# Opening of a fused two-model kernel: tokens loaded in two layouts, norms carried by the transform's table, modulation units in pairs, one order for the tensor engine

## The chip, the core and the metric

The kernel runs on one core of a Trainium2 chip. The metric is the device time of one whole execution, in microseconds (us). Smaller is better. The core has a tensor engine (PE), whose weight loads are listed apart as PEld, a vector engine (DVE), a scalar engine (ACT), GpSimd (POOL) and a sync engine (SP) that issues most transfers. Each engine works through its own queue of instructions in order.

## The reference

Two models run one after the other in single precision on a latent stream of 256 tokens and a context of 256 tokens, 1024 channels wide. The change touches the first layer of the first model only:

```python
silu_c, silu_cc = silu(c), silu(c_ctx)              # conditioning vectors, one per stream
for i in range(4):                                  # layers: fourier, diff attention, MLA, fourier
    sh_a, sc_a, g_a, sh_m, sc_m, g_m = split(silu_c @ mod_w[i] + mod_b[i], 6)     # csh_a ... from silu_cc
    h_lat = rms_norm(x_lat, norm_mix_g[i]) * (1 + sc_a) + sh_a                     # the context alike
    y_lat = mixer(h_lat)    # i = 0: real(fft2 over tokens and groups of 256 channels) @ fourier_w + bias
    x_lat = x_lat + g_a * y_lat
    h = rms_norm(x_lat, norm_mlp_g[i]) * (1 + sc_m) + sh_m
    x_lat = x_lat + g_m * (square(relu(h @ mlp_w1[i])) @ mlp_w2[i])
# then a second model: two layers of a state-space mixer beside attention, each with an MLP
```

## The kernel before

Activations lie with channels on the 128 partitions and the 512 tokens of both streams in columns (`self.x[k]`, k = 0 to 7). Every product of single precision is made of three products of rounded parts: a number is split into `hi` (a rounded cast on ACT) and `lo` (the rest, on DVE), and PE adds hi times hi, hi times lo and lo times hi. `split` (L396) does so for activations, `loadw` for weights: one transfer of 1 MB into a `raw` buffer (three of these), issued by SP at L288, then two casts `whi` on ACT (L306) and two rests `wlo` on DVE (L307). `whi` and `wlo` have five buffers each, the general tiles `g` 41, the accumulators `mm` and `aux` in PSUM four each.

**Modulation units.** The vectors sh_a to g_m of layer 0 are 24 units of 256 numbers for both streams: 0 to 3 are sh_a, 4 to 7 sc_a, 8 to 11 g_a, 12 to 15 sh_m, 16 to 19 sc_m, 20 to 23 g_m. `mod_land` loads 1 MB for a unit, into a `raw`, `whi`, `wlo` or `g` buffer. `mod_a` makes eight matmuls (L545, 16 records in the trace) into `aux` and lets ACT copy the result to `modsb` (L548). `mod_b` transposes it on PE (L556), and DVE sums it (L559) and adds the bias (L563). `mod_units` does the products of one unit ahead of the second half of the unit before. Units 20 to 23 are fed in among the MLP's first work. The other layers' vectors are made on DVE instead, by `mod_rows`: a row of silu(c) times a row of weights, summed (L588), beside PE's work; `rows_silu` makes that row first.

**The opening**, `start` (L883 to 1037). SP issues tokens, the first table, units 4 to 7, the second table and units 0 to 3. Each token's mean square is taken on ACT (L913); the normalised tokens are split (ACT L922, DVE L923); PE transposes the raw tokens into `self.x` (32 transposes, L930). The first transform is 96 matmuls (L946), whose sums are copied to `g` tiles (L951, L953). Then PE runs the eight units. Then ACT and DVE scale by 1 + sc_a and split (L980, L981), GpSimd writes two more columns for the shift sh_a (L976 for hi, L977 for lo), and PE makes the second transform (L995), 96 matmuls. Fourier weight tiles follow, units 8 to 11, 16 to 19 and 12 to 15, the last four output tiles in halves (`tail`), the norm, and the MLP's `head`, in which DVE makes one normalised tile for each k (L639, L643) and PE follows it with matmuls (L674 to 676). A plain `linear` (L324) is next.

A scheduler sets each engine's order, from the text and its own estimate of when operands are ready. `issue_after` forbids it to place work ahead of a named instruction.

Of the kernel before, what the change touches and what calls it, by code (L numbers as in the profile page):

```python
# [17 lines left out]
P = 128  # L18
# [105 lines left out]
def prep(inp):  # L124
    f = {k: np.asarray(v) for k, v in inp.items()}
    o = dict(_constants())
    o["xtok"] = np.concatenate([f["x"][0], f["ctx"][0]], axis=0).reshape(4, P, 2, 512).transpose(0, 2, 1, 3)
    o["cT"] = np.ascontiguousarray(
# [4 lines left out]
        DEPTH - 1, 24, P, 2 * D)  # L133
    o["mod_b"] = np.concatenate([_vecT(f["mod_b"][l]) for l in range(DEPTH)], axis=1)
# [107 lines left out]
class Body:  # L242
# [324 lines left out]
    def mod_units(self, units, dst, where="r"):  # L567

        prev = None
        for i, uu in enumerate(units):  # L570
            sb = self.mod_a(self.mod_land(uu, where[i % len(where)]))
            if prev:
                self.mod_b(*prev, dst)
            prev = (uu, sb)
            yield
        self.mod_b(*prev, dst)

    def mod_rows(self, l, ns, dst):


        nc = self.nc
        for cpt in (1, 0, 2, 4, 3, 5):
            for u in range(4):
                r = self.raw(self.I["mod_wT"][l - 1, cpt * 4 + u], 2048)
                c0 = cpt * 8 + u * 2
                for j in range(2):
                    for s in range(ns[cpt]):
                        nc.vector.tensor_tensor_reduce(  # L588
                            out=self.junk, in0=r[:, D * j:D * j + D], in1=self.silu_b[:, D * s:D * s + D],
                            scale=1.0, scalar=0.0, op0=ALU.mult, op1=ALU.add, accum_out=dst[:, c0 + j, s:s + 1])  # L590
                nc.vector.tensor_tensor(
                    out=dst[:, c0:c0 + 2, :ns[cpt]], in0=dst[:, c0:c0 + 2, :ns[cpt]],
                    in1=self.modb[:, l * 48 + c0:l * 48 + c0 + 2].unsqueeze(2).to_broadcast([P, 2, ns[cpt]]),
                    op=ALU.add)
                yield

# [286 lines left out]
    def start(self, mod):  # L883


        nc, I = self.nc, self.I
# [1351 lines left out]
```

## Time and profile before

| | us |
|---|---|
| three runs | 2946.76, 2953.48, 2955.89 |
| median of these | 2953.48 |
| the profiled execution: its time | 2948.07 |
| the profiled execution: its span | 2946.3 |

| engine | busy share of the span |
|---|---|
| PE | 97% |
| PEld | 88% |
| DVE | 73% |
| ACT | 51% |
| POOL | 1% |

Busy shares are means over the whole span. The first 165 us, which the change touches, look different: there the trace has to be read stretch by stretch, by what each engine waits for. [...]

### The profile page before, as it was taken

What the parts mean: (1) busy time and instruction counts of PE and PEld (TensorE: products, weight loads), DVE (VectorE), ACT (ScalarE), POOL (GpSimd) and SP (SyncE); (2) the same over time, 40 slices, a digit from 0 to 9 for tenths busy, and PEclk for the clock granted to TensorE, in tenths of its full rate; (3) what the DMA queues carried; (4) which work ended last, traced back from release to release, by engine and by line L of the source; (5) the groups of instructions that cost most, each with busy time, mean ns of one, the idle gap of its engine ahead of it and who ended that gap; (6) DMA issues with size and microseconds to landing.
All of it is one profiled execution on the core that took longest, in us unless ns stands there. A gap on an engine that the chain in (4) does not pass through costs nothing.

```text
span 2946.3 us, 51090 instructions
## 1 busy us (share of the span) xinstructions
PE 2863.0 (97%) x20316; PEld 2593.5 (88%) x20316; DVE 2153.2 (73%) x4707; ACT 1489.9 (51%) x2941; POOL 18.0 (1%) x66
## 2 busy tenths in 40 slices
PE   8999999998999999999999999999999999999999
PEld 6788889886888888599999999988999999989999
DVE  5597667775986667677756789886666799886765
ACT  5433323554432334855555567655554567655553
POOL 1000000000000000000000000000000000000000
PEclk9999999999999999999999999999999999999999
DMA  9454443320375553145525534333444444333553
GB/s 343 172 200 159 170 160 135 115 87 15 129 284 214 205 196 108 43 169 205 199 99 191 184 138 160 132 115 115 146 172 173 146 156 144 129 116 130 185 186 129
DMA packets 70366, 460.81 MB, mean 156 GB/s; under 512 B 7792, under 2 KB 9840, under 8 KB 16752
## 3 DMA queue, kind: packets, MB, share of 16 engines
q1 hardware_dynamic: 69984, 456.51, 43.6%
q8 instruction: 160, 2.62, 0.4%
q10 hardware_dynamic: 144, 1.05, 0.1%
q14 instruction: 78, 0.64, 0.1%
HBM read 456.47 MB, written 1.05 MB: 155 GB/s over the span
## 4 chain that ended last, share of the span: by engine, by line
PE 85%; DVE 8%; ACT 4%; DMA 1%; issue 1%; ACTq 0%; SPq 0%; DVEq 0%
PE mm L324 23%; PE mm L325 23%; PE mm L327 22%; DVE wlo L307 2%; ACT whi L306 1%; PE mm L675 1%; PE mm L674 1%; PE mm L676 1%; PE aux L1267 1%; PE mm L745 1%; PE aux L545 1%; PE mm L746 1%; PE mm L744 1%; DVE t L1701 1%; PE aux L1227 1%
## 5 line engine op out<-in xcount | busy, mean ns | idle before, releaser
L324 PE MATMUL mm<-g,whi 128*128 128x256 f32 (+3 forms) x5008 | 1406.9, 310 | 12.9 <-DVE t L1701 6.0
L325 PE MATMUL mm<-g,whi 128*128 128x256 f32 (+3 forms) x5008 | 1400.4, 308 | 0.5 <-DVE g L397 0.5
L306 ACT CAST whi<-raw 128x1024 fp32r<-128x1024 f32 (+2 forms) x670 | 697.5, 1048 | 821.0 <-PE mm L325 723.7
L324 PEld LDWEIGHTS mm<-g,whi 128*128 128x128 f32 x5008 | 941.6, 188 | 75.6 <-issue 15.7
L325 PEld LDWEIGHTS mm<-g,whi 128*128 128x128 f32 x5008 | 941.3, 188 | 51.7 <-issue 3.1
L307 DVE TENSOR_TENSOR wlo<-raw,whi 128x1024 fp32r<-128x1024 f32 (+2 forms) x670 | 809.5, 1210 | 122.0 <-ACT whi L306 65.7
L327 PE MATMUL mm<-g,wlo 128*128 128x256 f32 (+3 forms) x5008 | 835.2, 308 | 0.0
L327 PEld LDWEIGHTS mm<-g,wlo 128*128 128x128 f32 x5008 | 712.8, 188 | 47.0 <-issue 0.7
L588 DVE CUSTOM_DVE_ANT_0 junk<-raw,silu_b 128x1024 bf16<-128x1024 f32 x208 | 253.8, 1220 | 46.8 <-DMA raw<-in_mod_wT 44.9
L607 DVE SCALAR_TENSOR_TENSOR x<-mm,mod,x 128x256 f32<-128x256 f32 x216 | 98.3, 479 | 129.1 <-PE mm L327 125.4
L769 DVE TENSOR_TENSOR y<-mm,rb 128x256 f32<-128x256 f32 (+1 forms) x144 | 61.3, 427 | 89.8 <-PE mm L327 68.5
L846 DVE TENSOR_TENSOR g<-t,g 128x256 fp32r<-128x256 f32 (+2 forms) x192 | 98.5, 514 | 4.2
L843 ACT ACTIVATE t<-t 128x256 f32<-128x256 f32 (+2 forms) x192 | 94.0, 491 | 8.0 <-DVE g L846 2.9
L1701 DVE SCALAR_TENSOR_TENSOR t<-mm,cwh,t 128x270 f32<-128x270 f32 (+2 forms) x192 | 91.9, 490 | 2.7 <-ACT t L1698 2.4
L2195 DVE TENSOR_TENSOR x<-x,mm 128x272 f32<-128x272 f32 (+1 forms) x64 | 27.5, 429 | 81.0 <-PE mm L327 81.0
L675 PE MATMUL mm<-g,whi 128*128 128x256 f32 x240 | 66.7, 287 | 1.7 <-DVE g L643 1.6
L676 PE MATMUL mm<-g,wlo 128*128 128x256 f32 x240 | 65.5, 282 | 0.0
L841 ACT ACTIVATE t<-mm 128x512 f32<-128x512 f32 x64 | 37.9, 600 | 53.7 <-PE mm L327 53.6
L845 DVE CAST g<-t 128x256 fp32r<-128x256 f32 (+2 forms) x192 | 64.0, 334 | 1.3 <-ACT t L843 0.9
L674 PE MATMUL mm<-g,whi 128*128 128x256 f32 x240 | 60.7, 285 | 2.6 <-ACT g L642 2.6
L744 PE MATMUL mm<-g,whi 128*128 128x258 f32 (+2 forms) x192 | 54.5, 287 | 1.0 <-ACT g L716 0.7
L745 PE MATMUL mm<-g,whi 128*128 128x258 f32 (+2 forms) x192 | 54.7, 286 | 0.3 <-DVE g L717 0.3
(409 smaller groups left out, 3270.9 us busy)
## 6 DMA issues: line engine op xcount, KB each, us to landing
raw<-in_mlp_w SPq DMA_DIRECT2D x128, 1024.0 KB, 4.9
raw<-in_w_in SPq DMA_DIRECT2D x76, 1024.0 KB, 4.9
raw<-in_mod_wT SPq DMA_DIRECT2D x72, 1024.0 KB, 4.9
raw<-in_w_up SPq DMA_DIRECT2D x32, 1024.0 KB, 4.8
raw<-in_w_dn SPq DMA_DIRECT2D x32, 1024.0 KB, 4.8
raw<-in_diff_w SPq DMA_DIRECT2D x16, 1024.0 KB, 4.8
raw<-in_w_sd SPq DMA_DIRECT2D x16, 1024.0 KB, 4.8
raw<-in_mod_w SPq DMA_DIRECT2D x13, 1024.0 KB, 5.3
```

The costliest lines, as they stand in the source:

```text
L306: nc.scalar.copy(hi, v)
L307: nc.vector.tensor_tensor(out=lo, in0=v, in1=hi.bitcast(F32), op=ALU.subtract)
L324: mm(ps, w(0, k, c0, c1), xs[k][0], start=first and k == 0, stop=False)
L325: mm(ps, w(0, k, c0, c1), xs[k][1], start=False, stop=False)
L327: mm(ps, w(1, k, c0, c1), xs[k][0], start=False, stop=last and k == n - 1)
L588: nc.vector.tensor_tensor_reduce(out=self.junk, in0=r[:, D * j:D * j + D], in1=self.silu_b[:, D * s:D * s + D], scale=1.0, scalar=0.0, op0 ...
L607: self.nc.vector.scalar_tensor_tensor(out=self.x[m][:, c0:c1], in0=ps[:, c0:c1], scalar=mod[:, gc * 8 + m, s:s + 1], in1=self.x[m][:, c0:c ...
L675: mm(pss[i][:, c0:c1], w(0, k, o, o + P), l, start=False, stop=False)
L676: mm(pss[i][:, c0:c1], w(1, k, o, o + P), h, start=False, stop=k == 7)
L843: nc.scalar.activation(s[:, :n], t[:, :n], AF.Square)
L846: nc.vector.tensor_tensor(out=lo, in0=s[:, :n], in1=hi.bitcast(F32), op=ALU.subtract)
L1701: nc.vector.scalar_tensor_tensor(out=t[:, sft:L2], in0=ps[:, :L2 - sft], scalar=cw[:, 3 - sft:4 - sft], in1=t[:, sft:L2], op0=ALU.mult, op ...
```

## The change

**Tokens.** A second input, `xT`, holds the tokens with channels on partitions, and is loaded into `self.x`; the 32 transposes and their copies go. The raw tokens are split as they come; the mean squares are shared between ACT and DVE. The factor 1/rms of a token goes into the first table instead, which is scaled and split once for each block of 128 tokens.

**Transform.** The first transform's sums are scaled by 1 + sc_a and split straight from PSUM, with no copy between. Units 4 to 7 therefore come before it; two of its eight tiles (`early`) are made before unit 7. Units 0 to 3 follow it.

**Units** come in twos: products of two, then the second halves of the two. Units 20 to 23 are made on DVE from a transposed copy of their weights (`mod_wT0`). The factor 0.5 of silu moves from the row into the reductions.

**Order.** Inside `start`, PE's matmuls and transposes keep the order of the text. The two fourier weights are loaded ahead of the second transform, and the units of g_a, sc_m and sh_m are placed between output tiles.

```diff
+    o["xT"] = np.concatenate([f["x"][0], f["ctx"][0]], axis=0).T.reshape(KT, P, NF)
+    o["mod_wT0"] = f["mod_w"][0].reshape(D, 24, 2, P).transpose(1, 3, 2, 0).reshape(24, P, 2 * D)[20:24]
...
-    def mod_units(self, units, dst, where="r"):
-        prev = None
-        for i, uu in enumerate(units):
-            sb = self.mod_a(self.mod_land(uu, where[i % len(where)]))
-            if prev:
-                self.mod_b(*prev, dst)
-            prev = (uu, sb)
+    def mod_units(self, units, dst):
+        for i in range(0, len(units), 2):
+            sbs = [(uu, self.mod_a(ld)) for uu, ld in units[i:i + 2]]
             yield
-        self.mod_b(*prev, dst)
+            for uu, sb in sbs:
+                self.mod_b(uu, sb, dst)
+            yield
...
+    def in_order(self):
+        nc, keep = self.nc, self.tc.keep_in_program_order
+        ctx = ExitStack()
+        for nm_ in ("matmul", "transpose"):
+            f = getattr(nc.tensor, nm_)
+            setattr(nc.tensor, nm_, lambda *a, f=f, **k: keep(f(*a, **k)))
+            ctx.callback(delattr, nc.tensor, nm_)
+        return ctx
...
+    def mod_row(self, ap, l, c0, ns, dst):
+        nc = self.nc
+        r = self.raw(ap, 2048)
+        for j in range(2):
+            for s in range(ns):
+                nc.vector.tensor_tensor_reduce(
+                    out=self.junk, in0=r[:, D * j:D * j + D], in1=self.silu_b[:, D * s:D * s + D],
+                    scale=0.5, scalar=0.0, op0=ALU.mult, op1=ALU.add, accum_out=dst[:, c0 + j, s:s + 1])
+        nc.vector.tensor_tensor(
+            out=dst[:, c0:c0 + 2, :ns], in0=dst[:, c0:c0 + 2, :ns],
+            in1=self.modb[:, l * 48 + c0:l * 48 + c0 + 2].unsqueeze(2).to_broadcast([P, 2, ns]), op=ALU.add)
+    def mod_last(self, dst):
+        for u in range(4):
+            self.mod_row(self.I["mod_wT0"][u], 0, 40 + u * 2, 2, dst)
+            yield
...
-        units = [4, 5, 6, 7, 0, 1, 2, 3]
-        lands = [self.mod_land(uu, wh) for uu, wh in zip(units[:4], "rrrh")]
-        c2 = []
+            t = self.g()[:, :258]
+            nc.sync.dma_start(t, I["dft1"][kk])
+            t1.append(t)
+        def land(uus, where):
+            return [(uu, self.mod_land(uu, wh)) for uu, wh in zip(uus, where)]
+        lands1 = land(range(4, 8), "rrrh")
+        t2 = []
         for i in range(2):
             t = self.g()
             nc.sync.dma_start(t[:, :512], I["dft2"][i])
-            c2.append(t)
-        lands += [self.mod_land(uu, wh) for uu, wh in zip(units[4:], "hllg")]
-        xn = {}
-        for s in range(2):
-            ss = self.sm(4)
-            for i in range(4):
+            t2.append(t)
+        mod0 = self.mod_units(land(range(0, 4), "hllg"), mod)
...
+                if h:
+                    nc.vector.tensor_tensor_reduce(out=sq, in0=x, in1=x, scale=1.0, scalar=0.0, op0=ALU.mult,
+                                                   op1=ALU.add, accum_out=ss[:, c:c + 1])
+                else:
+                    nc.scalar.activation(sq, x, AF.Square, accum_out=ss[:, c:c + 1])
...
+        for tt in range(4):
+            hi, lo = self.pair(258)
+            a_c1 = nc.scalar.activation(hi, t1[tt % 2], AF.Copy, scale=r[:, tt:tt + 1])
+            v_c1 = nc.vector.scalar_tensor_tensor(out=lo, in0=t1[tt % 2], scalar=r[:, tt:tt + 1], in1=hi.bitcast(F32),
+                                           op0=ALU.mult, op1=ALU.subtract)
+            c1.append((hi, lo))
...
-        for k in range(KT):
-            ps = self.mm()
-            for tt in range(4):
-                nc.tensor.transpose(ps[:, tt * P:tt * P + P], xk[tt, k // 4][:, (k % 4) * P:(k % 4) * P + P], self.ident)
-            if k % 2:
-                nc.scalar.copy(self.x[k], ps)
-            else:
-                nc.vector.tensor_copy(self.x[k], ps)
...
+        def uev(k, pss):
+            hi, lo = self.g(F32R), self.g(F32R)
+            h4, l4 = [t.rearrange("p (c q) -> p c q", c=2) for t in (hi, lo)]
+            for s, ps in enumerate(pss):
                 v = ps[:, :258].rearrange("p (c u) -> p c u", u=129)
-                if s:
-                    nc.scalar.copy(o, v)
-                else:
-                    nc.vector.tensor_copy(o, v)
-            uv.append(t)
-        with self.tc.issue_after(last.ins), self.tc.issue_after(mlast.ins):
-            prev = None
-            for uu, ld in zip(units, lands):
-                sb = self.mod_a(ld)
-                if prev:
-                    self.mod_b(*prev, mod)
-                prev = (uu, sb)
-            self.mod_b(*prev, mod)
-        c2 = [self.split(t[:, :512]) for t in c2]
-        asc = self.norm_scale(0, 1, 0, mod)
+                sl = slice(129 * s, 129 * s + 129)
+                nc.scalar.activation(h4[:, :, sl], v, AF.Copy, scale=asc[:, k, s:s + 1])
+                nc.vector.scalar_tensor_tensor(out=l4[:, :, sl], in0=v, scalar=asc[:, k, s:s + 1],
+                                               in1=h4[:, :, sl].bitcast(F32), op0=ALU.mult, op1=ALU.subtract)
+            us.append((hi, lo))
+        with self.tc.issue_after(a_c1.ins), self.tc.issue_after(v_c1.ins):
+            sbs = []
+            for i, (uu, ld) in enumerate(lands1):
+                if i == 3:
+                    early = [umm(0), umm(1)]
+                sbs.append((uu, self.mod_a(ld)))
+                if i:
+                    self.mod_b(*sbs[i - 1], mod)
+            self.mod_b(*sbs[3], mod)
+            asc = self.norm_scale(0, 1, 0, mod)
+            for k in range(KT):
+                uev(k, early[k] if k < 2 else umm(k))
+        self.drain(mod0)
...
-            nc.gpsimd.tensor_copy(h4[:, 0, 258:260], shh[:, k, :])
-            nc.gpsimd.tensor_copy(l4[:, 0, 258:260], shl[:, k, :])
...
+            nc.gpsimd.tensor_copy(us[k][0][:, 258:260], shh[:, k, :])
+            nc.gpsimd.tensor_copy(us[k][1][:, 258:260], shl[:, k, :])
         fs = []
+        ws = [self.loadw(I["fourier_w"][0, u], 8, 256) for u in range(2)]
+        mod2 = self.mod_units(land(range(8, 12), "gggg"), mod)
+        for k in range(KT):
+            nc.sync.dma_start(self.x[k], I["xT"][k])
...
+        mod4 = self.mod_units(land(range(16, 20), "gggg"), mod)
+        self.drain(mod2)
-        self.drain(self.mod_units([8, 9, 10, 11], mod, "rggr"))
...
+        mods = self.chain(mod4, self.mod_units(land(range(12, 16), "gggg"), mod))
+        for m in range(4):
+            ps = self.mm()
+            self.mm3(ps, ws[m // 2], m % 2 * P, m % 2 * P + P, fs)
+            ev(m, ps)
+            if m:
+                next(mods)
+            next(mods)
+            if m == 2:
+                self.nb.asc = self.norm_scale(0, 4, 4, mod)
+        self.drain(mods)
+        self.drain(self.tail([I["fourier_w"][0, u] for u in (2, 3)], fs, ev, 4))
...
-            nc.vector.tensor_scalar(out=v, in0=v, scalar1=0.5, scalar2=None, op0=ALU.mult)
...
-                    self.start(mod)
+                    with self.in_order():
+                        self.start(mod)
...
-                         self.mod_units([20, 21, 22, 23], mod) if l == 0 else iter(()))
+                         self.mod_last(mod) if l == 0 else iter(()))
```

In the orders below a name's first number counts the buffers of its kind and the second the program's instructions.

ACT's queue in the opening, before: copies of the units' products (`modsb` 107 and 111 are the fourth and fifth of the eight units, `raw_201` is the first fourier weight).

```order
L548 COPY modsb_107_515<-aux_106_506 128x256
L548 COPY modsb_111_532<-aux_110_523 128x256
L306 CAST whi_202_872<-raw_201_870 128x1024
L980 ACTIVATE g_136_613<-g_72_325,nsc_132_605 128x2x129
L548 COPY modsb_115_549<-aux_114_540 128x256
L980 ACTIVATE g_136_613<-g_72_325,nsc_132_605 128x2x129
L306 CAST whi_204_876<-raw_201_870 128x1024
```

The same place after: `modsb` 62, 64, 68 and 76 are units 4, 5, 6 and 7, `raw_133` and `raw_138` are the two fourier weights, `mm_71` and `mm_72` the first tile of the first transform.

```order
L550 COPY modsb_62_275<-aux_61_266 128x256
L550 COPY modsb_64_286<-aux_63_277 128x256
L308 CAST whi_134_596<-raw_133_594 128x1024
L550 COPY modsb_68_303<-aux_67_294 128x256
L308 CAST whi_136_600<-raw_133_594 128x1024
L550 COPY modsb_76_348<-aux_75_339 128x256
L308 CAST whi_139_606<-raw_138_604 128x1024
L980 ACTIVATE g_82_364<-mm_71_311,nsc_81_362 128x2x129
L980 ACTIVATE g_82_364<-mm_72_318,nsc_81_362 128x2x129
```

The casts of the first weight now stand ahead of the copies of units 6 and 7, and one of the second weight ahead of the first evacuation.

GpSimd's queue at the shift columns, before:

```order
L976 COPY g_136_613<-shh_134_609 128x2
L977 COPY g_137_614<-shl_135_610 128x2
L976 COPY g_138_621<-shh_134_609 128x2
L977 COPY g_139_622<-shl_135_610 128x2
L976 COPY g_140_629<-shh_134_609 128x2
```

And after:

```order
L1007 COPY g_100_450<-shh_131_574 128x2
L1007 COPY g_104_470<-shh_131_574 128x2
L1007 COPY g_108_490<-shh_131_574 128x2
L1008 COPY g_83_365<-shl_132_575 128x2
L1008 COPY g_85_371<-shl_132_575 128x2
```

A tile's low column stood right behind its high one; now the high columns come first, and the first low one behind the last of them (eight in all).

DVE's queue in the MLP's head, before: the normalisations of k = 6 and 7 and the first reduction for layer 1 (`raw_424`).

```order
L643 SCALAR_TENSOR_TENSOR g_252_1093<-t_391_1742,mod0_125,g_251_1092 128x256
L639 SCALAR_TENSOR_TENSOR t_404_1815<-x6_100,nsc_297_1229,aux_351_1548 128x256
L643 SCALAR_TENSOR_TENSOR g_254_1095<-t_397_1777,mod0_125,g_253_1094 128x256
L639 SCALAR_TENSOR_TENSOR t_407_1837<-x7_101,nsc_297_1229,aux_351_1548 128x256
L643 SCALAR_TENSOR_TENSOR g_256_1097<-t_404_1815,mod0_125,g_255_1096 128x256
L588 ISA junk_134,mod1_126<-raw_424_1973,silu_b_133 128x1024
L588 ISA mod1_126 128x1
L643 SCALAR_TENSOR_TENSOR g_258_1099<-t_407_1837,mod0_125,g_257_1098 128x256
```

The head after, at k = 3 and 4 (`raw_381` and `raw_383` are the weights of two g_m units, lines 659 and 663 the old 639 and 643):

```order
L659 SCALAR_TENSOR_TENSOR t_382_1658<-x3_97,nsc_301_1181,aux_350_1509 128x256
L423 SCALAR_TENSOR_TENSOR r_377_1621<-rt_379_1623,r_377_1621 128x2
L604 ISA junk_134,mod0_125<-raw_381_1651,silu_b_133 128x1024
L604 ISA mod0_125 128x1
L663 SCALAR_TENSOR_TENSOR g_248_956<-t_382_1658,mod0_125,g_247_955 128x256
L607 TENSOR_TENSOR mod0_125<-mod0_125,k0_85 128x4
L604 ISA junk_134,mod0_125<-raw_383_1674,silu_b_133 128x1024
L604 ISA mod0_125 128x1
L659 SCALAR_TENSOR_TENSOR t_384_1681<-x4_98,nsc_301_1181,aux_350_1509 128x256
L604 ISA junk_134,mod0_125<-raw_383_1674,silu_b_133 128x1024
L604 ISA mod0_125 128x1
L663 SCALAR_TENSOR_TENSOR g_250_958<-t_384_1681,mod0_125,g_249_957 128x256
```

Reductions for units 20 to 23 now stand between the normalisations.

## Rows read from the trace of the kernel before

**Rows 1.** The page: engines' busy shares, and the chain that ended last

```profile
PE 2863.0 (97%) x20316; PEld 2593.5 (88%) x20316; DVE 2153.2 (73%) x4707; ACT 1489.9 (51%) x2941; POOL 18.0 (1%) x66
PE 85%; DVE 8%; ACT 4%; DMA 1%; issue 1%; ACTq 0%; SPq 0%; DVEq 0%
```

**Rows 2.** Windows: from:to, length, engines' busy us (count), clock, DMA share, GB/s

```profile
0.00:34.00 34.00, 22.46 (x132) 19.38 (x136) 16.81 (x57) 18.14 (x41) 1.37 (x12) 0.90 0.95 371
34.00:36.00 2.00, 2.00 (x34) 1.06 (x34) 0.93 (x2) 0.83 (x3) 0.00 (x0) 1.00 0.04 14
...
20.00:24.00 4.00, 3.71 (x17) 3.72 (x18) 4.00 (x8) 1.61 (x3) 0.00 (x0) 0.50 1.04 409
```

**Rows 3.** Timeline of SP's queue: start us, length us, the first fourier weight's issue

```profile
35.05 1.19 SPq L288 DMA_DIRECT2D raw<-in_fourier_w  x2
```

**Rows 4.** Timeline of ACT: the cast of the first fourier weight

```profile
40.35 1.05 ACT L306 CAST whi<-raw 128x1024 fp32r<-128x1024 f32 x1
```

**Rows 5.** ACT, 7 to 55 us, by form: busy us, mean ns | idle

```profile
L548 ACT COPY modsb<-aux 128x256 f32<-128x256 f32 x9 | 3.4, 374 | 5.0 <-PE aux L545 5.0
...
L396 ACT CAST g<-g 128x512 fp32r<-128x512 f32 x2 | 1.1, 622 | 0.0
...
L396 ACT CAST g<-g 128x258 fp32r<-128x258 f32 x2 | 0.8, 401 | 0.0
```

**Rows 6.** Timeline of PE: start us, length us, count, [wait before <- engine]

```profile
20.29 4.45 PE L946 MATMUL mm<-g,g 128*128 128x258 f32 x19 [0.31 <-DVE g L923]
...
24.99 9.00 PE L946 MATMUL mm<-g,g 128*128 128x258 f32 x72 [0.25 <-ACT g L951]
...
36.15 1.07 PE L545 MATMUL aux<-raw,silu_c 128*32 128x256 f32 x16
...
37.52 1.07 PE L545 MATMUL aux<-whi,silu_c 128*32 128x256 f32 x16
...
48.38 6.32 PE L995 MATMUL mm<-g,g 128*128 128x260 f32 x36 [1.88 <-POOL g L976]
...
62.79 0.40 PE L324 MATMUL mm<-g,whi 128*128 128x512 f32 x1
...
85.08 1.07 PE L545 MATMUL aux<-g,silu_c 128*32 128x256 f32 x16
```

**Rows 7.** DVE, 7 to 66 us, by form

```profile
L559 DVE TENSOR_REDUCE sm<-aux 128x4 f32<-128x16 f32 x8 | 1.4, 172 | 4.5 <-PE aux L556 4.5
...
L307 DVE TENSOR_TENSOR wlo<-raw,whi 128x1024 fp32r<-128x1024 f32 x4 | 4.9, 1219 | 0.5 <-ACT whi L306 0.5
```

**Rows 8.** Timeline of POOL: the first high and the last low shift column

```profile
47.90 0.43 POOL L976 CAST g<-shh 128x2 fp32r<-128x2 f32 x1 [40.70 <-DVE shl L970]
...
53.84 0.45 POOL L977 CAST g<-shl 128x2 fp32r<-128x2 f32 x1
```

**Rows 9.** Waits of PE, 0 to 230 us: sum, count, longest in us

```profile
PE aux L556 <- ACT modsb L548: 5.2, 4, 3.9
```

**Rows 10.** Timeline of PE: slow unit, tail's last half tile, head, next linear

```profile
98.53 1.94 PE L545 MATMUL aux<-raw,silu_c 128*32 128x256 f32 x16
...
128.91 0.28 PE L324 MATMUL mm<-g,whi 128*128 128x256 f32 x1
...
131.72 0.28 PE L674 MATMUL mm<-g,whi 128*128 128x256 f32 x1
...
162.54 0.39 PE L324 MATMUL mm<-g,whi 128*128 128x512 f32 x1
```

**Rows 11.** Window over the head, columns as in rows 2

```profile
134.00:163.00 29.00, 28.23 (x263) 25.43 (x264) 28.26 (x77) 15.02 (x29) 0.00 (x0) 1.00 0.52 192
```

**Rows 12.** DVE, 134 to 163 us, by form: the scaling of silu

```profile
L1518 DVE TENSOR_SCALAR silu_b<-silu_b 128x512 f32<-128x512 f32 x4 | 1.7, 419 | 0.0
```

**Rows 13.** Timeline of DVE: the first reduction for layer 1

```profile
157.65 1.22 DVE L588 CUSTOM_DVE_ANT_0 junk<-raw,silu_b 128x1024 bf16<-128x1024 f32 x1
158.80 0.08 DVE L588 DVE_READ_ACCUMULATOR2_ANT mod<- 128x1 f32 x1
```

More of the change, by code (lines that the diff above doesn't have):

```diff
@@ L583, in mod_rows @@
             for u in range(4):
[L584 to L594, printed above, removed]
-                yield
+                self.mod_row(self.I["mod_wT"][l - 1, cpt * 4 + u], l, cpt * 8 + u * 2, ns[cpt], dst)
+                yield
+    def mod_row(self, ap, l, c0, ns, dst):
[13 more added lines that the diff above has]
+            yield
     def norm_scale(self, l, comp, gidx, mod):
@@ new lines, in start @@
+        ss = self.sm(8)
+        xs = {}
+        for tt in range(4):
+            for h in range(2):
+                x = xk[tt, h]
+                xs[tt, h] = self.split(x)
+                c = 2 * tt + h
+                sq = self.tp.tile([P, 512], F32, tag="sq", name=self.nm("sq"), bufs=2)
+                if h:
[3 more added lines that the diff above has]
+                    nc.scalar.activation(sq, x, AF.Square, accum_out=ss[:, c:c + 1])
@@ new lines, in start @@
+        s2 = self.sm(4)
+        nc.vector.tensor_reduce(out=s2, in_=ss.rearrange("p (t h) -> p t h", h=2), axis=AX.X, op=ALU.add)
+        r = self.sm(4)
+        self.rstd_of(s2, r, 1.0 / D)
+        c1 = []
+        for tt in range(4):
+            hi, lo = self.pair(258)
[3 more added lines that the diff above has]
+            c1.append((hi, lo))
@@ L939, in start, with umm @@
+        def umm(k):
+            pss = []
             for s in range(2):
@@ L942, in start @@
                 for tt in range(2):
-                    xh, xl = xn[2 * s + tt, k // 4]
+                    xh, xl = xs[2 * s + tt, k // 4]
+                    ch, cl = c1[2 * s + tt]
                     sl = slice((k % 4) * P, (k % 4) * P + P)
-                    for a, b in ((xh, c1[tt][0]), (xh, c1[tt][1]), (xl, c1[tt][0])):
-                        mlast = mm(ps[:, :258], a[:, sl], b, start=first, stop=tt == 1 and a is xl)
+                    for a, b in ((xh, ch), (xh, cl), (xl, ch)):
+                        mm(ps[:, :258], a[:, sl], b, start=first, stop=tt == 1 and a is xl)
@@ L965, in start @@
+        self.drain(mod0)
+        c2 = [self.split(t[:, :512]) for t in t2]
         sh16 = self.vp.tile([P, KT, 2], F32, tag="gb", name=self.nm("sh16"), bufs=2)
```

58 lines of the change are left out of this document (7 added, 51 removed).

## The prediction

> **What bounds the kernel now.** I read the page's shares and its chain first: the tensor engine (PE) is busy 97% of the span and holds 85% of the chain that ended last [rows 1]. So a delay of PE in the opening is not caught up later unless PE has idle time behind it, and it has little. The change touches the first 165 us only. There I read four things: when the bytes land, what stands in the scalar engine's (ACT's) queue, where PE waits, and how full the vector engine (DVE) is.
>
> The transfers come first. In the first 34 us the queues move 371 GB/s, 12.6 MB, and then stop for nearly two us [rows 2]. That is exactly what is issued before the first fourier weight (constants 0.30, silu vector 1.05, tokens 2.10, first table 0.26, eight modulation units 8.39, second table 0.52 MB). The fourier weight is issued at 35.05 [rows 3], because its buffer is held by a unit that PE reads at 34, and ACT casts it at 40.35 [rows 4], by then between unit copies that PE does not miss. PE runs the first transform to 34, the eight units to 46.5, the second transform from 48.38 to 62.8 [rows 6], four output tiles to 85, then modulation units with 5.2 us of waits for ACT's copies [rows 9], then the tail until 131.7, where the MLP's head begins; the next plain linear begins at 162.54 [rows 10]. I call the start of the head E. In the head DVE is busy 28.26 of 29 us [rows 11].
>
> **The change part by part.**
>
> *Transposes and token split.* The 32 transposes and 8 copies to `x` go; `x` comes by 2.1 MB of transfers instead. PE did them while it waited for tokens. I cost both at nothing: the cover is the wait for the units' bytes, and `x` is first needed after 79 us in the new order, though it lands by about 44 (estimate: 2.1 MB behind 14.7 MB at 0.4 MB/us).
>
> *ACT's queue.* This is the term that decides the opening. In the new order the cast of the first fourier weight stands ahead of the copy for unit 6, its second half ahead of the copy for unit 7, and the second weight's first half ahead of every evacuation of the first transform. The weight's buffer is now free early, but its transfer stands behind the same 12.6 MB, which drain at about 33.6 [rows 2]. At 0.4 MB/us the first weight lands at 36.2 and the second at 38.8. ACT gets there long before: the last odd token square near 12, eight casts of about 0.57 (the two shown took 1.1 in all), four table scalings of 0.4, two copies of 0.37 [rows 5], so at 19. It then stands for 17 us. Behind it: unit 6's copy, on which PE's next transpose waits; PE may not pass it, because its order is now the text's. PE has done both early transform tiles and unit 7 by 27 and stands too.
>
> From 36.2: cast 1.05 [rows 4], copy 0.37, cast 1.05, copy 0.37: 39.0. PE transposes unit 7 by 39.4, DVE sums and scales by 40.2 (three operations of about 0.2 [rows 7]); ACT's third cast ends at 40.1. ACT and DVE evacuate the first tile, and PE goes on at 41.4. Three quarters of the transform remain, 72 matmuls, which took 9.00 [rows 6]. PE has idled, and after an idle stretch the granted clock was 0.50 in 20 to 24 [rows 2], where 19 matmuls took 4.45 instead of 2.4 [rows 6]: 2.1 more. So 52.5. Evacuation (ACT 0.4 a tile by the same form's row [rows 5], DVE taken as the like) is hidden under PE's 0.75, six of those matmuls; if that cover were gone it would cost nothing beyond the last tile.
>
> Four units, 1.37 each (36.15 to 37.52 in steps of one unit) [rows 6], and two waits of about 0.3 where two transposes now follow two products: 58.6. A weight cast of 1.22 [rows 7] stands in DVE between the last sum and the last bias, and then the three shift operations: 61.3. On GpSimd all eight high shift columns now stand ahead of the first low one; 16 casts took 53.84 - 47.90 and one more [rows 8], 0.40 a piece, so PE waits 3.2 + 0.4 for the first low one: 64.8. The second transform took 14.4, from 48.38 to 62.79, with its own slow start [rows 6]: it ends at 79.1, **16.3 late**.
>
> *Behind the transform.* PE then needs four units at 1.37 with two waits of 0.5 (6.5), four output tiles (22.3, 62.79 to 85.08), eight units (11.0) and one wait (0.5), eight half tiles of the tail at 2.81 (128.91 to 131.72 [rows 10]: 22.5) and 1.0 for the norm: 63.8, so E is 142.9. Before, this took 68.9, because of the 5.2 us of waits [rows 9] and products at half speed behind them (1.94 for one unit at 98.53, 1.07 at full speed [rows 10]). The new order gives back 5.1: **E is 11.2 late**. The transfers of these units are hidden: their buffers come free by 84, before their turn at 91 to 114.
>
> *The four gate units on DVE.* Units 20 to 23 leave PE, 4 x 1.37 = 5.5 us, and become 16 reductions on DVE of 1.15 net (1.22 long, 157.65 to 158.80) [rows 12, 13]. In the built order these 16 stand between the head's normalisations, one or two to each k, and three of layer 1's before the last normalisation, where it was five in all. So 14 more times 1.15 is 16.1, plus four bias adds 0.3, less four silu scalings 1.5 (0.42 long [rows 12]) and the old units' small sums 0.8: the last normalisation, which before ended where the next reduction begins, at 157.65, E + 25.9 [rows 13], comes at E + 40.0. PE follows the normalisations k by k, with 15 matmuls left behind the last one, 1.8: E + 41.8. It was 162.54, E + 30.8 [rows 10]: **11.0 more**, after the 5.5 us saved on PE, since PE idles in that stretch. I take the head's DVE order as it stands. The bounds of this term are 0 (PE's old 30.8 us hide all of it) and 16.1 (nothing that was removed counts).
>
> [...]
>
> *Without effect:* the factor 0.5 moved into the reductions, and pairs of units as such.
>
> Sum: 11.2 + 11.0 = 22.2. The profiled run's own time is 2948.07, so 2970.3. The median of the three runs shown is 2953.48, 5.4 above it; I put the forecast halfway, **2973**.
>
> **The rivals.**
>
> *Weights in time.* If the first weight landed before ACT asks for it (by about 20 us), the 17 us of standing vanish. Then PE is bound by unit 7's bytes: the transform resumes near 30, ends near 39.5, units to 46, shift columns and the low casts to 51, second transform to 65, E 2.5 early, head 11 late: 8.5 more, 2957 (2959 from halfway). It needs the transfers out of order or twice as fast; 0.95 busy share at 371 GB/s [rows 2] speaks against it.
>
> *Only PE's own time counts* (the other side). If every removed wait were a gain and every new one hidden: 5.5 us of units, 5.2 of waits and 2.8 of half speed behind them, 13.5 less, 2935 (2937 from halfway). It decides from the point where DVE has 18 us free under the head. The row for 134 to 163 leaves 0.7 [rows 11], and that speaks against it. [...] In the head the trace has DVE as the fuller engine.
>
> *The reductions cost nothing.* The queue stands, but the reductions slip beside other work: 11.2 more, 2959 to 2962. Against it is DVE's order, which is fixed.
>
> *More than that.* PE also runs the second half of the head at the lower clock (up to 2.1 for the restart), and DVE enters the next linear with four reductions undone (up to 4.6): 22 + 7 = 29 more, 2977 to 2982.
>
> **How the numbers follow.** Forecast 0.64, weights in time 0.10, PE alone 0.07, reductions free 0.12, more than that 0.07. The range, 2958 to 2984, holds the forecast (with either base, 2970 to 2976, and errors of 6 each way), the free reductions and the worse case, and leaves out the rest of the two small rivals. About 0.3%, 9 us, is what a measurement of this kernel can tell from no change. Faster by that: 0.07. Within: 0.08, from the weights in time. Slower: 0.85.
>
> **What would show it.** In the new profile: ACT idle from about 19 to 36 for a transfer of the fourier weight; PE idle before a transpose of unit 6 until 37 or 38; PE waiting about 3.5 us for GpSimd's low column; second transform ending near 79; no wait of 3.9 us behind the output tiles; E near 143; PE waiting for DVE throughout the head, with the next linear near 185. The forecast is wrong if ACT does not wait for the weight, or if PE's idle time in the head is below 5 us.

## The result: slower by 0.65%, and the profile after

| | before | after |
|---|---|---|
| median, us | 2951.91 (5 runs) | 2971.45 (5 runs, 2966.64 to 2977.83) |
| ratio | | 1.0065, 95% interval 1.0048 to 1.0083 |
| profiled execution: time, span | 2948.07, 2946.3 | 2966.72, 2964.9 |

The change costs 19.5 us between the medians and 18.6 between the two profiled spans. The forecast was 2973, that is 19.5 above the median it was set against.

The page's shares and its chain hardly move (they answer to [rows 1]): PE is busy for 9.3 us less, and the span is 18.6 longer.

```profile
PE 2853.7 (96%) x20212; PEld 2587.6 (87%) x20212; DVE 2165.5 (73%) x4717; ACT 1482.1 (50%) x2919; POOL 13.5 (0%) x66
...
PE 85%; DVE 8%; ACT 4%; DMA 2%; issue 1%; SPq 0%; POOL 0%; ACTq 0%; DVEq 0%
```

The loss has two places. The first is ACT's queue. In its timeline (start, length, [wait before <- engine]) the copies of units 4 and 5 are done at 20.1, and ACT then waits 16.99 us for the first fourier weight. Before, that cast started at 40.35 [rows 4], and from 30 to 62 us PE waited for a copy of ACT's only once, 0.5 us.

```profile
19.75 0.37 ACT L550 COPY modsb<-aux 128x256 f32<-128x256 f32 x1 [1.73 <-PE aux L585]
37.12 1.04 ACT L308 CAST whi<-raw 128x1024 fp32r<-128x1024 f32 x1 [16.99 <-DMA raw<-in_fourier_w]
38.07 0.36 ACT L550 COPY modsb<-aux 128x256 f32<-128x256 f32 x1
```

SP had issued that weight at 28.12, 7 us earlier than before [rows 3], but behind the same bytes:

```profile
28.12 1.60 SPq L290 DMA_DIRECT2D raw<-in_fourier_w  x2
```

PE's timeline shows the wait passed on (it answers to [rows 6]). PE finishes unit 7's products at 25.6 and stands 12.90 us for unit 6's copy, which is the one that starts at 38.07 above. The first transform's last 72 matmuls then run from 42.19, the second transform from 61.48 to 75.34, and the next work starts there instead of at 62.79.

```profile
24.52 1.07 PE L585 MATMUL aux<-whi,silu_c 128*32 128x256 f32 x16
38.49 0.69 PE L585 MATMUL aux<-k,modsb 128*128 128x128 f32 x2 [12.90 <-ACT modsb L550]
...
42.19 11.02 PE L585 MATMUL mm<-g,g 128*128 128x258 f32 x72 [1.80 <-DVE g L981]
...
62.47 7.26 PE L585 MATMUL mm<-g,g 128*128 128x260 f32 x58 [0.47 <-POOL g L1008]
70.49 4.92 PE L585 MATMUL mm<-g,g 128*128 128x260 f32 x36 [0.76 <-DVE t L1034]
75.34 1.93 PE L585 MATMUL aux<-g,silu_c 128*32 128x256 f32 x32
```

The second place is the MLP's head, which begins at 140.38 (131.72 before [rows 10]) and ends at 181.88 (162.54 before):

```profile
140.38 0.28 PE L694 MATMUL mm<-g,whi 128*128 128x256 f32 x1
...
181.88 0.50 PE L326 MATMUL mm<-g,whi 128*128 128x512 f32 x1
```

In the windows over the head (columns as in rows 2; the clock is PE's granted one, as a share of full speed) DVE is busy all 29.00 us from 153 to 182, and PE 21.97 of them:

```profile
140.40:150.00 9.60, 6.08 (x33) 5.29 (x32) 9.16 (x26) 4.11 (x8) 0.00 (x0) 0.79 0.25 100
150.00:153.00 3.00, 3.00 (x17) 3.00 (x16) 3.00 (x10) 0.51 (x1) 0.00 (x0) 0.54 0.00 0
153.00:182.00 29.00, 21.97 (x157) 19.13 (x157) 29.00 (x62) 8.55 (x16) 0.00 (x0) 1.00 0.45 150
```

DVE's timeline there shows why: normalisation (L659, L663), reduction (L604), normalisation, reduction, with no gap. Each reduction delays the next tile that PE waits for.

```profile
155.17 0.48 DVE L663 SCALAR_TENSOR_TENSOR g<-t,mod,g 128x256 fp32r<-128x256 f32 x1
155.57 1.22 DVE L604 CUSTOM_DVE_ANT_0 junk<-raw,silu_b 128x1024 bf16<-128x1024 f32 x1
...
156.71 0.47 DVE L659 SCALAR_TENSOR_TENSOR t<-x,nsc,aux 128x256 f32<-128x256 f32 x1
157.10 1.22 DVE L604 CUSTOM_DVE_ANT_0 junk<-raw,silu_b 128x1024 bf16<-128x1024 f32 x1
```

And the waits of PE from 120 to 420 us (sum, count, longest) are two rows of this kind, where before the head had 0.6:

```profile
PE mm L694 <- ACT g L662: 7.3, 7, 2.5
PE mm L695 <- DVE g L663: 2.6, 8, 0.7
```

The last of these waits ends at 173.65; from there PE has work without a gap until the next linear:

```profile
173.65 0.38 PE L695 MATMUL mm<-g,whi 128*128 128x256 f32 x1 [0.66 <-DVE g L663]
```

From the next linear on, the two kernels take the same: 2946.3 - 162.54 = 2783.8 before, 2964.9 - 181.88 = 2783.0 after.

### The profile page after: what moved, and what is told of

The parts are those of the page before. It is cut to its first block, busy times and chain, and to the rows that moved or that the text cites. A ratio compares the mean times of both kernels' runs of the same rounds, so it can differ in the third digit from the quotient of the medians.

```text
span 2964.9 us, 50931 instructions
## 1 busy us (share of the span) xinstructions
PE 2853.7 (96%) x20212; PEld 2587.6 (87%) x20212; DVE 2165.5 (73%) x4717; ACT 1482.1 (50%) x2919; POOL 13.5 (0%) x66
## 3 DMA queue, kind: packets, MB, share of 16 engines
q10 hardware_dynamic: 144, 1.05, 0.1%
HBM read 458.57 MB, written 1.05 MB: 155 GB/s over the span
## 4 chain that ended last, share of the span: by engine, by line
PE 85%; DVE 8%; ACT 4%; DMA 2%; issue 1%; SPq 0%; POOL 0%; ACTq 0%; DVEq 0%
PE mm L326 23%; PE mm L327 23%; PE mm L329 22%; PE mm L585 2%; DVE wlo L309 2%; DVE junk L604 1%; PE mm L765 1%; PE mm L766 1%; PE mm L695 1%; PE aux L1291 1%; PE mm L764 1%; ACT whi L308 1%; PE mm L694 1%; PE mm L696 1%; PE aux L1962 1%
## 5 line engine op out<-in xcount | busy, mean ns | idle before, releaser
L326 PE MATMUL mm<-g,whi 128*128 128x256 f32 (+4 forms) x4912 | 1378.6, 310 | 13.4 <-DVE t L1725 6.1
L327 PE MATMUL mm<-g,whi 128*128 128x256 f32 (+4 forms) x4912 | 1373.2, 308 | 0.5 <-DVE g L399 0.5
L326 PEld LDWEIGHTS mm<-g,whi 128*128 128x128 f32 (+1 forms) x4912 | 923.8, 188 | 74.2 <-issue 13.3
L327 PEld LDWEIGHTS mm<-g,whi 128*128 128x128 f32 (+1 forms) x4912 | 923.5, 188 | 49.4 <-issue 3.1
L309 DVE TENSOR_TENSOR wlo<-raw,whi 128x1024 fp32r<-128x1024 f32 (+2 forms) x670 | 810.2, 1211 | 150.4 <-ACT whi L308 82.5
L329 PE MATMUL mm<-g,wlo 128*128 128x256 f32 (+3 forms) x4912 | 818.5, 308 | 0.0
L329 PEld LDWEIGHTS mm<-g,wlo 128*128 128x128 f32 x4912 | 698.5, 188 | 46.2 <-issue 0.7
L604 DVE CUSTOM_DVE_ANT_0 junk<-raw,silu_b 128x1024 bf16<-128x1024 f32 x224 | 273.6, 1221 | 50.6 <-DMA raw<-in_mod_wT 48.8
L789 DVE TENSOR_TENSOR y<-mm,rb 128x256 f32<-128x256 f32 (+1 forms) x144 | 61.4, 428 | 90.1 <-PE mm L329 68.9
L861 ACT ACTIVATE t<-mm 128x512 f32<-128x512 f32 x64 | 37.8, 597 | 52.6 <-PE mm L329 52.5
L662 ACT ACTIVATE g<-t,mod 128x256 fp32r<-128x256 f32 x64 | 30.5, 506 | 60.3 <-DVE t L659 60.1
L764 PE MATMUL mm<-g,whi 128*128 128x258 f32 (+2 forms) x192 | 54.6, 287 | 0.7 <-ACT g L736 0.7
```

Source lines behind the costliest of these rows:

```text
L309: nc.vector.tensor_tensor(out=lo, in0=v, in1=hi.bitcast(F32), op=ALU.subtract)
L326: mm(ps, w(0, k, c0, c1), xs[k][0], start=first and k == 0, stop=False)
L327: mm(ps, w(0, k, c0, c1), xs[k][1], start=False, stop=False)
L329: mm(ps, w(1, k, c0, c1), xs[k][0], start=False, stop=last and k == n - 1)
L604: nc.vector.tensor_tensor_reduce(out=self.junk, in0=r[:, D * j:D * j + D], in1=self.silu_b[:, D * s:D * s + D], scale=0.5, scalar=0.0, op0 ...
```

## The experiments

The theory: (1) ACT's queue stands behind a cast whose transfer has not landed, PE stands behind ACT, and nothing later gives this back; (2) the 16 reductions stand in DVE's queue between normalisations on which PE waits. All kernels are the changed one with a small edit, except e5 and e10, which are the kernel before with one part of the change. The diffs are shortened, with instructions named in words. Times of PE's timeline, in us:

| kernel | work behind the second transform starts | head starts | next linear | median | ratio to before (95%) |
|---|---|---|---|---|---|
| before | 62.79 | 131.72 | 162.54 | 2951.91 | |
| after | 75.34 | 140.38 | 181.88 | 2971.45 | 1.0065 |
| e1, casts behind the evacuations | 66.08 | 131.00 | 172.53 | 2961.61 | 1.0040 (1.0026 to 1.0054) |
| e2, units 20 to 23 on PE | 78.21 | 143.25 | 173.77 | 2967.63 | 1.0054 (1.0042 to 1.0067) |
| e3, reductions behind the head | 75.22 | 140.22 | 171.20 | 2965.77 | 1.0055 (1.0041 to 1.0068) |
| e4, e1 and e3 | 65.90 | 130.76 | 161.09 | 2957.18 | 1.0022 (1.0013 to 1.0031) |
| e5, before, with the reductions | 62.50 | 129.59 | 171.16 | 2963.18 | 1.0026 (1.0015 to 1.0038) |
| e6, no text order | 82.45 | 145.67 | 187.76 | 2972.16, one run | |
| e7, e1 and the later casts | 62.54 | 127.57 | 169.08 | 2959.79 | 1.0027 (1.0015 to 1.0039) |
| e8, e7 and e2 | 63.01 | 128.03 | 158.55 | 2944.78 | 0.9976 (0.9965 to 0.9987) |
| e9, tokens ahead of the weights | 81.09 | 146.11 | 187.62 | 2972.50, one run | |
| e10, before, without transposes | 63.31 | 130.44 | 161.25 | 2953.63 | 0.9996 (0.9984 to 1.0008) |

(In e6 other work stands between the second transform's matmuls.) Each ratio is to runs of the kernel before taken beside that kernel; their medians were 2951.91 (after), 2949.62 (e1 to e4), 2953.04 (e7, e8) and 2953.47 (e5, e10).

### e1: only the place of the casts

```diff
+        with issue_after(last evacuation on ACT), issue_after(last evacuation on DVE):
             ws = [self.loadw(I["fourier_w"][0, u], 8, 256) for u in range(2)]
```

> The changed kernel with one thing moved: the casts of the first two fourier weights are issued on ACT and DVE behind the last evacuation of the first transform; the transfers stay where they are. Theory (ACT's queue stands behind a cast whose transfer has not landed): ACT's 17.0 us of idle time for the fourier weight goes, unit 6's transpose starts near 24 instead of 38.5, the first transform resumes near 29 and ends near 39, the second ends near 62 instead of 75.3, the MLP's head starts near 127 instead of 140.4: 13 less in all, some 2958. Rival (the bytes are the limit, and the cast only shows it): units 0 to 3 or the casts behind them now wait, the second transform ends at 70 or later and less than 6 us are gained.

The 17.0 us are gone from ACT, and the first transform resumes at 28.23 instead of 42.19, 14 earlier. But only 9.4 of that reach the head. PE's timeline shows a new wait, 6.45 us for GpSimd's shift columns:

```profile
28.23 10.41 PE L585 MATMUL mm<-g,g 128*128 128x258 f32 x72 [1.80 <-DVE g L981]
...
51.68 0.80 PE L585 MATMUL mm<-g,g 128*128 128x260 f32 x2 [6.45 <-POOL g L1008]
```

It is the same fault one weight later. ACT waits for the third fourier weight, DVE for ACT's cast, and behind its rest (L309) stands the bias of unit 3 (L565, at 50.80), on which the shift columns depend. ACT's row and DVE's:

```profile
48.58 1.04 ACT L308 CAST whi<-raw 128x1024 fp32r<-128x1024 f32 x1 [3.84 <-DMA raw<-in_fourier_w]
```

```profile
49.66 1.23 DVE L309 TENSOR_TENSOR wlo<-raw,whi 128x1024 fp32r<-128x1024 f32 x1 [3.44 <-ACT whi L308]
50.80 0.15 DVE L565 TENSOR_TENSOR mod<-sm,k 128x4 f32<-128x4 f32 x1
```

The theory holds for the first wait; the size of 13 was wrong because I had not followed the queue to the third weight.

### e7: the later casts too

```diff
+        self.hold = nc.vector.tensor_tensor(out=shl, ...)      # last shift operation
 ...
     def tail(self, aps, xs, evac, m0):
+        with issue_after(self.hold):
             ws = [self.loadw(ap, 8, 256) for ap in aps]
```

> As e1, and the third and fourth fourier weight's casts and rests are also held, behind the last of the three shift operations on DVE. In e1 the rest of the third weight, whose transfer landed at 48.6, stood on DVE ahead of unit 3's bias, and PE waited 6.45 us for the shift columns. Theory (one more case of a queue that stands behind a transfer): that wait falls to some 2 us, as in the changed kernel, the second transform ends near 61.5 instead of 66.1, the head starts near 126.5 instead of 131.0 and the next linear near 168 instead of 172.5; the whole 4.5 less than e1, some 2957. Rival (the shift columns wait for the rests of the first two weights and the sums anyway): the second transform ends later than 64.5.

The wait for the shift columns falls to 1.91 us, and the second transform starts at 46.91 instead of 51.68:

```profile
46.91 0.80 PE L585 MATMUL mm<-g,g 128*128 128x260 f32 x2 [1.91 <-POOL g L1012]
47.89 9.56 PE L585 MATMUL mm<-g,g 128*128 128x260 f32 x58 [0.18 <-POOL g L1013]
```

The head starts at 127.57, 12.8 earlier than in the changed kernel and 3.4 earlier than in e1 (expected 4.5). The rest went into the second transform, which took 14.65 us from 47.89; in e1 it took 13.42 and in the changed kernel 12.87, at a granted clock of 1.00. Here the granted clock was 0.81 from 46 to 64. The edit is not needed for that: e2 (below), whose opening is that of the changed kernel, has 0.81 there too, from 60 to 78.2. The windows over both second transforms, of the changed kernel and of e7:

```profile
60.00:76.00 16.00, 13.22 (x108) 12.28 (x112) 9.91 (x30) 6.12 (x14) 2.03 (x16) 1.00 0.67 244
```

```profile
46.00:64.00 18.00, 16.61 (x124) 15.28 (x128) 11.07 (x32) 7.47 (x16) 2.03 (x16) 0.81 1.01 377
```

### e9 and e6: the dose, and PE's order

e9 moves a transfer:

```diff
-        ws = [self.loadw(...) for u in range(2)]
         for k in range(KT):
             nc.sync.dma_start(self.x[k], I["xT"][k])
+        ws = [self.loadw(...) for u in range(2)]
```

> The changed kernel with the 2.1 MB of tokens for the residual stream moved ahead of the fourier weights on the transfer queue, nothing else. Theory (ACT stands until the first weight has landed, and PE behind it): the weight lands some 5.4 us later, near 42.5; unit 7's transpose, which follows the casts, starts near 45 instead of 39.7, and the head starts 5 us later, near 145.5. Rival (something else holds the first transform until 42 anyway): the head starts within 1.5 us of 140.4.

The weight's cast moves from 37.12 to 42.20: 2.1 MB more cost 5.1 us, 0.41 MB/us. Unit 7's transpose moves from 39.70 to 44.52, the second transform's first matmul by 4.2 and the head by 5.7; 1.5 of this is that transform's first 58 matmuls, which took 8.81 us instead of 7.26. So the delay passes through. The scheduler put unit 6's copy ahead of the cast here, so PE's long wait, 18.90 us, is for unit 7's.

```profile
42.20 1.99 ACT L308 CAST whi<-raw 128x1024 fp32r<-128x1024 f32 x2 [20.73 <-DMA raw<-in_fourier_w]
```

```profile
44.52 0.69 PE L585 MATMUL aux<-k,modsb 128*128 128x128 f32 x2 [18.90 <-ACT modsb L550]
```

e6 lets the scheduler order PE:

```diff
-                    with self.in_order():
-                        self.start(mod)
+                    self.start(mod)
```

> The changed kernel without the text's order for PE: the scheduler places PE's matmuls. Theory (ACT's queue is the cause, and PE's order only passes it on): PE still stands some 13 us for unit 6's copy, and the head starts within 3 us of 140.4. Rival (the fixed order of PE is the cause): that wait falls below 5 us, and the head starts 5 or more earlier.

PE waits until the same 38.5. The wait is 10.33 us now because the matmuls before it, 92 as in the changed kernel, end at 28.2 instead of 25.6. The head starts 5.3 later, not within 3 (the second transform's first 58 matmuls took 8.79 us here, 1.5 more): the free order is the worse one in this run. So the fixed order is not the cause.

```profile
38.55 0.69 PE L558 MATMUL aux<-k,modsb 128*128 128x128 f32 x2 [10.33 <-ACT modsb L550]
```

### e2: units 20 to 23 on PE again

```diff
-                         self.mod_last(mod) if l == 0 else iter(()))
+                         self.gates(mod) if l == 0 else iter(()))     # mod_a and mod_b, one unit to a step
```

> The changed kernel with units 20 to 23 made by PE again, as before the change, one to a step of the head. Theory (the 16 reductions lengthen DVE's order in the head, and PE follows DVE): from the head's first matmul to the next plain linear 30.8 us as before the change instead of 41.5, 10.7 less in all, some 2961. Rival (PE saves 5.5 us of units, and the head is long because it starts at another place beside other transfers): it stays at 38 or more, and the time falls by less than 4.

The head takes 30.52 us, against 41.50: 11.0 less, as the theory has it.

```profile
143.25 0.28 PE L705 MATMUL mm<-g,whi 128*128 128x256 f32 x1
...
173.77 0.40 PE L326 MATMUL mm<-g,whi 128*128 128x512 f32 x1
```

The whole gained only 3.8 in the medians, and 3.4 between the profiled spans. Of the difference, 2.9 lies ahead of the head: mainly, the second transform's first 58 matmuls took 9.54 us instead of 7.26, on the same instructions. The other 4.7 lie behind the next linear, in stretches of lower clock at places where the kernel before has 1.00, as from 1850 to 1900 (e2, before, and e10, where the code is that of the kernel before):

```profile
1850.00:1900.00 50.00, 47.51 (x381) 46.06 (x381) 44.53 (x103) 31.52 (x77) 0.00 (x0) 0.93 0.31 106
```

```profile
1850.00:1900.00 50.00, 47.20 (x402) 45.83 (x401) 47.26 (x107) 35.41 (x94) 0.00 (x0) 1.00 0.32 111
```

```profile
1850.00:1900.00 50.00, 47.50 (x382) 46.05 (x381) 45.16 (x102) 34.55 (x93) 0.00 (x0) 0.93 0.31 106
```

So e2's edit is not what lowers the clock there. From PE's longest wait in layer 1 (4.49 us, at 686.68 before) to the end, the profiled executions take 2259.0 to 2259.8 us (before, after, e3, e6, e8, e9) or 2263.9 to 2267.5 (the other six), though no edit touches that part. Two profiled spans can differ by 8 us from this alone; why is open.

### e3 and e4: the reductions held back

```diff
-            if i >= 2:
-                next(early, 0)
-            if i >= start:
-                self.rows_add(rate)
+            if i >= 18:                                   # layer 0; the head has 18 steps
+                with issue_after(last normalisation):
+                    next(early, 0)
+                    self.rows_add(rate)
```

> The changed kernel with all reductions of the head, those of units 20 to 23 and those of layer 1, held on DVE behind the last normalisation. Theory (the place in DVE's order is what costs, not the work): the head takes what PE needs, 24 to 27 us instead of 41.5, the linear behind it covers the reductions, and 15 less in all, some 2956. Rival (the work itself is too much for DVE, which is 97% busy in the next 46 us): PE waits in the linear or the next ones for the held work, and no more than 5 are gained.

The head fell to 30.98 us, not to 24 to 27, although no reduction is left ahead of its last normalisation, which ends at 161.25. PE's rows show what the units on PE had done there. Without them PE idles 1.47 and 2.54 around the norm, and after that its granted clock is 0.56 and 0.75 for ten us (windows, columns as in rows 2):

```profile
143.75 0.61 PE L438 MATMUL aux<-ones,sqa 128*128 128x1 f32 x4 [1.47 <-DVE sqa L645]
146.90 1.22 PE L694 MATMUL mm<-g,whi 128*128 128x256 f32 x4 [2.54 <-ACT g L662]
```

```profile
145.00:150.00 5.00, 3.10 (x14) 3.10 (x15) 4.96 (x21) 2.23 (x6) 0.00 (x0) 0.56 0.00 0
150.00:155.00 5.00, 5.00 (x35) 5.00 (x34) 3.71 (x9) 2.17 (x5) 0.00 (x0) 0.75 0.00 2
```

In the kernel before, three of the four units stand in that very gap, and the window over the head has 1.00 [rows 11]:

```profile
134.18 0.60 PE L436 MATMUL aux<-ones,sqa 128*128 128x1 f32 x4 [0.88 <-DVE sqa L625]
134.72 1.93 PE L545 MATMUL aux<-raw,silu_c 128*32 128x256 f32 x32
...
136.95 1.07 PE L545 MATMUL aux<-raw,silu_c 128*32 128x256 f32 x16
```

So the 5.5 us that the change took from PE were worth nothing: with the units gone, PE waits in their place and then runs slower, at the 0.56 and 0.75 above. The work held back (layer 1's reductions, too, start at step 18 of the head instead of step 12) then came due at layer 1's own head of normalisations. There reductions stand in the way again, as in DVE's row, and PE waits 2.87 and slows once more, to a granted clock of 0.83 from 500 to 520 (1.00 before):

```profile
509.69 0.61 PE L438 MATMUL aux<-ones,sqa 128*128 128x1 f32 x4 [0.86 <-DVE sqa L645]
513.16 1.22 PE L694 MATMUL mm<-g,whi 128*128 128x256 f32 x4 [2.87 <-ACT g L662]
```

```profile
510.81 1.23 DVE L604 CUSTOM_DVE_ANT_0 junk<-raw,silu_b 128x1024 bf16<-128x1024 f32 x1
```

From the next linear to PE's longest wait in layer 1 it is 524.1 us before, 523.3 after, and 530.6 in e3: 7.3 lost there. In the kernels without this edit it is 523.0 to 524.1.

e4 is e3 with e1's edit:

> Both edits: the casts behind the evacuations, and the reductions behind the head. If the two costs are separate and PE never idles to win them back, the gains add: 28 less than the changed kernel, some 2943, which is 8 to 9 less than the kernel before (0.3%). Rival: what the opening gains is lost at the head or in the linears behind it, where DVE is nearly full; then it is not below the better of the two alone.

The two gains add up to the next linear (161.09, that is 20.8 less than the changed kernel; 9.4 and 10.7 alone), and 7 are lost again by layer 1 (530.3). It is not below the kernel before.

### e8: the version that beats both

e8 is e7 with e2's edit.

> e7 with units 20 to 23 on PE again. Theory: the head takes 30.6 us as in e2, from the same start as e7, so the next plain linear is near 157 to 159, 3 to 5 us earlier than in the kernel before (162.54), and the time is some 2945 to 2947, just below it. In e3 and e4 the reductions held back came due at layer 1's first norm (7 us from the next linear to the end of layer 1's attention); here nothing is held, so nothing is due. Rival (the units on PE cost their 5.5 us wherever DVE leaves room): the next linear is at 162 or later.

The head takes 30.52 us with the granted clock at 1.00, the next linear starts at 158.55, 4.0 earlier than in the kernel before, and the ratio is 0.9976 (0.9965 to 0.9987): about 7 us faster than before and 27 faster than the change as it stands. Between the profiled spans it is 5.5, and 4.0 of that is the opening; where the rest comes from was not traced.

```profile
128.00:158.50 30.50, 29.88 (x274) 26.49 (x273) 28.41 (x75) 16.47 (x33) 0.00 (x0) 1.00 0.57 205
```

### e5 and e10: one part of the change alone

e5 puts units 20 to 23 on DVE in the kernel before (`mod_last`, and the factor 0.5 moved):

> The kernel before with one part of the change alone: units 20 to 23 as 16 reductions on DVE, and the factor 0.5 moved. Theory (the reductions stand between the normalisations, and the units on PE filled time in which PE waits for the norm anyway): the head starts at 131.7 as before and takes 41.5 us, the next linear is near 173 instead of 162.5, and the time is 10 to 11 more, some 2960 to 2962. Rival (the 5.5 us that PE saves count): 5 or less more.

The head takes 41.57 us, from 129.59 to 171.16: 10.8 more, the forecast's 11.0. PE's waits in it are 8.0 and 3.1:

```profile
PE mm L684 <- ACT g L652: 8.0, 7, 2.5
```

The median is 9.7 above that of the runs beside it, and the ratio gives 7.7, where 10 to 11 were expected. Between the profiled spans it is 16.3, for e5's execution is one of the six longer ones named under e2. Its head started 2.1 earlier than in the profiled run of before, in a stretch that the edit does not touch: from the second transform to the head both e5 and e10 take 67.1 us, and before took 68.9. Behind PE's 3.9 us wait for a copy the granted clock was 1.00 from 100 to 132 in these two, and 0.94 before.

e10 replaces the transposes of the kernel before by the transfer of `xT`, behind the first two fourier weights:

```diff
-        for k in range(KT):                       # 32 transposes and 8 copies
-            ...
+        with issue_after(second fourier weight's transfer):
+            for k in range(KT):
+                nc.sync.dma_start(self.x[k], I["xT"][k])
```

> The kernel before with one part of the change alone: the residual stream's tokens come by a transfer behind the first two fourier weights, and the 32 transposes and their copies are gone. The prediction costs this at nothing, since PE made the transposes while it waited for the tokens. Theory: the second transform ends within 1.5 us of 62.8 and the head starts within 2 of 131.7. Rival (PE, without the transposes, idles and runs the first transform longer at the lower clock): it ends 2 to 4 later. Rival (PE's work counts): it ends 2 to 4 earlier.

The work behind the second transform starts at 63.31 (62.79 before), the head at 130.44, and the ratio is 0.9996. Neither rival shows: PE's 32 transposes were free.

## Why the prediction was right, point by point

**The transposes at nothing.** Right by e10.

**ACT's queue, 16.3 late at the second transform's end.** The mechanism was right: unit 6's copy, whose products PE had ended at 21.3, ran at 38.07, right behind the cast. The size was 12.5 (75.34 against 62.79). The first steps came within 1 us each: the weight's cast at 37.12 (forecast 36.2, at 0.4 MB/us), the first transform going on at 42.19 (41.4) and ending at 53.1 (52.5). Two terms were too large. GpSimd's columns: I took 0.40 us a cast from [rows 8], so 3.6 us from the shift operations to the second transform's start; it was 1.1 (61.37 to 62.47), and PE's wait for the first low column 0.47. The eight high casts took 1.05 and the eight low ones 1.04:

```profile
61.23 1.05 POOL L1007 CAST g<-shh 128x2 fp32r<-128x2 f32 x8 [53.80 <-DMA g<-in_mod_w]
62.23 1.04 POOL L1008 CAST g<-shl 128x2 fp32r<-128x2 f32 x8
```

And the second transform: 14.4 by [rows 6], where it began slowly (a granted clock of 0.73 from 47.90 to 54.30); it took 12.9 here, at a granted clock of 1.00.

**What the new order gives back.** 5.1 by the forecast, 3.9 by the trace: 68.9 us before from the second transform to the head, 65.0 now. The 5.2 us of waits of [rows 9] are gone, but PE now waits for the units' copies between the output tiles, three times 0.70, 0.52, 0.30 and 0.20, 3.1 in all, where I had 1.5. And 1.8 of the 3.9 depends on the execution, since the old order takes 67.1 in e5 and e10. So the head is 8.7 late, not 11.2. The two errors, 3.8 too much and 1.2 too little, left 2.5.

**The reductions, 11.0.** Measured 10.7 (41.50 - 30.82), 10.8 in e5 and 11.0 in e2. The order of DVE's queue, read row by row, gave this within half a us: the last normalisation ends at E + 39.0 (179.42), where E + 40.0 was forecast.

```profile
178.55 0.87 DVE L663 SCALAR_TENSOR_TENSOR g<-t,mod,g 128x256 fp32r<-128x256 f32 x2
```

The end of the head was seen less well. PE does not follow DVE to the last tile: it waits last at 173.65, and has 2.5 us of work behind the last normalisation, not 1.8. The bounds of 0 and 16.1 were not needed. The row shown as [rows 13] is not the first reduction for layer 1 but the sixth; the five that the prediction counts stand ahead of it.

**The rivals.** Weights in time: e7 is that case by another road (the casts out of the way), and its head starts 4.2 earlier than before; the rival had 2.5. Only PE's own time counts: dead by e3, where PE has its 5.5 us less and the head takes no less than before. PE is the busiest engine over the whole span (96% in the changed kernel), yet the head took 10.8 us more when units 20 to 23 left PE in e5, and 11.0 less when they came back in e2: in the changed kernel's head DVE was busy all 29.00 us from 153 to 182. Reductions free: dead by e2 and e5. More than that: the granted clock did fall in the head, but in its first part, to 0.79 from 140.4 to 150 and 0.54 from 150 to 153; it was 1.00 from there to 182, with PE busy 21.97 of 29.00 us. By 154.70 PE was waiting for the next tile again, so the 3.08 to 3.16 us from one tile to the next (L663 in DVE's timeline, 152.01 to 170.71) hid it; and the next linear lost nothing by the reductions still undone (2783.0 us to the end, 2783.8 before).

**The sum.** 22.2 forecast, 18.6 in the spans (8.7 and 10.7, less 0.8 behind the head); 2970.3 against 2966.72 for the profiled run. That the median of after lies only 1.5 from the forecast is partly luck: it is 4.7 above its own profiled run.

## What to carry to other kernels

Before a load is moved forward in the text, look where its cast lands in the queue of the engine that casts it: here a cast ahead of its bytes held ACT and what stood behind it for 16.99 us, and what helped was to move the cast, not the transfer. Work taken off the busiest engine is worth only what that engine would not have idled in its place; the small products that filled PE's waits were cheap here (a head of 30.82 us with them, 30.98 without them in e3), and the engine they are moved to may be the one that is waited for, as DVE was (41.50). Read such orders row by row, and follow a queue past the first stall: the next one took 3.4 of the 12.8 us that mending the first could give.

## What the runs showed of the hardware that I had not expected

GpSimd's small casts (128x2) took 0.40 us apart in the kernel before and 0.13 in the changed one. Before, DVE ran 16 scalings beside them (L981, 6.45 us for 16, so 0.40 each), and the casts kept step with them, one to one; in the changed kernel DVE was idle. In e10 the first cast, at 46.19, takes 0.19, and from the third on, at 46.66, they are 0.40 apart.

```profile
46.19 0.19 POOL L968 CAST g<-shh 128x2 fp32r<-128x2 f32 x1 [38.97 <-DVE shh L961]
46.39 0.32 POOL L969 CAST g<-shl 128x2 fp32r<-128x2 f32 x1
46.66 0.46 POOL L968 CAST g<-shh 128x2 fp32r<-128x2 f32 x1
```

GpSimd has no wait on record between the casts. That DVE's scalings slow them is what I make of these rows; no run changes the scalings alone, so it is argued, not shown. What the runs do show is that I had taken a duration beside DVE's scalings, 0.40 us, for the work's own, and it was 0.13 with DVE idle.
